# A two-layer diffusion trunk on one core: row sums of the modulations spread over the program, a wider apply of the norm, and caches loaded from another queue

## The chip, the cores and the metric

The kernel runs on one core of a Trainium2 chip, as one program and one launch. The metric is the device time of an execution in microseconds (us): here the median of three runs. The engines have short names below: PE is TensorE, DVE VectorE, ACT ScalarE, POOL GpSimd, SP SyncE. Each engine takes its instructions in the order in which the program issues them. A transfer is issued by the queue of an engine, and the issue stands in that engine's order like any other instruction.

## The reference

Two layers run over 128 context tokens and 128 latent tokens, with D = 1024 channels and D_FF = 2816. Each layer is two half feed-forward steps around a mixer:

```
x += 1/2 * gate1 * SwiGLU_1(mod1(RMSNorm(x)))
u  = mod2(RMSNorm(x)); z = u @ W_in
branches on z: differential attention, 2-D DFT, bidirectional chunkwise mLSTM
x += gate2 * (sum of gated branches @ W_out)
x += 1/2 * gate3 * SwiGLU_2(mod3(RMSNorm(x)))
modulation (shift, scale, gate) x 3 = SiLU(cond) @ W_ada + b_ada
```

`mod` is `x * (1 + scale) + shift`. The nine modulations of a layer are products of one vector for each token group with nine 1024 x 1024 blocks of `W_ada`. Latent tokens also read cached context keys and values (`cache_k`, `cache_v`) and seed the mLSTM from `state_C`. Everything is fp32, and the outputs are the two token groups, the new caches and the new states.

## The kernel before

All activations stay on chip, channels on the 128 partitions, both token groups side by side (256 columns). What moves is the weights, 1 MB chunks through six buffers called `raw`, each issued on SP's queue. A chunk is used as two or more **units** of 128x1024. Every unit is split into a high and a low part: ACT casts it (`whi`, L1473) and DVE subtracts the cast from the original (`wlo`, L1474). A product is then three matmuls, `hi*hi`, `lo*hi` and `hi*lo` (L167 to L169), so that PE, ACT and DVE all work on every unit. Splits are made up to six units ahead of use.

The program is a Python list, `steps`. A step has a function that issues its matmuls and follow-up work, and the units that it needs; the list's order is each engine's order. A layer has the parts ffn1 (22 blocks of the hidden width in 11 pairs, the "in" part, then four pairs of output channels, the "out" part), the mixer (queries first, then keys, values and the others, three branches, the output product), and ffn2.

Three places matter for the change.

**Modulations.** 16 of the 18 modulations are made while other parts run (the first two in `begin`). Seven are *row sums* on DVE: a chunk of the transposed weight is multiplied with the conditioning vector, broadcast over the partitions (`cb`), and summed over a row, in 16 instructions of 128x1024 per modulation (L339). Nine go through PE as *side steps*: 16 matmuls each, with the 32 columns of the conditioning vectors on the stationary side, two side steps a modulation (L164), and a `post` step of four transposes per part that has any. The table `ADA` (L42 to L47) gives for each part which modulations are row sums and which go through PE, and `spread_into` (L1288) spreads all of them evenly over the part's steps. Nearly all row sums stand in the "in" parts, since `spread_into` covers only these in an ffn.

**The norm.** `Norm` first makes `y = x * scale` block by block and splits it (`yh`, `yl`), so that the first four units of the next part can be multiplied by `y` before the norm's sum of squares is known. Then `stats`, `root` (a power on POOL), `diag` and `spread` make `bcs`, the reciprocal root for each token on all partitions, and `apply` (L478 to L491) makes `u = x * bcs * scale + shift` in eight blocks of 128x256, one multiplication on POOL (the first on DVE) and one half-block each on ACT and DVE, followed by a split into `uh` on ACT and `ul` on DVE. All units after the first four multiply by `u`.

**The start of a mixer.** After the queries' step, `loads2` (L676 to L682) issues three loads on POOL's queue: `cache_k` and `cache_v` into `ckv`, `state_C` into `C`. The attention's work runs as a lane, pieces of it issued between the matmuls of the following units: its first PE work is four transposes of `ckv` (L787), two and a half units after the first one that multiplies by `u`.

`begin` is ffn1 of the first layer: the first two modulations arrive in slabs (`ada(j)`, `channel(j)`) and the first three pairs are multiplied channel block by channel block.

Of the kernel before, what the change touches and what calls it, by code (L numbers as in the profile page):

```python
# [14 lines left out]
ALU = mybir.AluOpType  # L15
# [24 lines left out]
CT = 8  # L40
# [76 lines left out]
class Step:  # L117
    def __init__(self, fn, units=(), pump=True, lanes=False, ahead=()):
        self.fn, self.units, self.pump, self.lanes = fn, list(units), pump, lanes
        self.ahead = list(ahead)  # L120


@with_exitstack
def trunk_kernel(ctx: ExitStack, tc: tile.TileContext, a: dict):
# [89 lines left out]
    cb = const.tile([P, 2, D], F32, name="cb")  # L214
    maskb = const.tile([P, 2, P], BF16, name="maskb")
# [3 lines left out]
    run = {"lanes": False}  # L219
    late, held = [], []  # L220

    def add(fn, units=(), pump=True, ln=False, ahead=()):
        steps.append(Step(fn, units, pump, ln, ahead))

# [71 lines left out]

    def mod_steps(mods_):
# [4 lines left out]

        on_ve, mods_ = mods_
        st = {"left": 4 * len(mods_)}
        seq = []
# [12 lines left out]
        def finish(l, m, o, x):  # L318
            bT = parT[l][:, m * KD:(m + 1) * KD].unsqueeze(2).to_broadcast([P, KD, 2])
            ve.tensor_add(o, x, bT)  # L320
            if m % 3 == 1:
                k0 = 72 + m // 3 * KD
                gT = parT[l][:, k0:k0 + KD].unsqueeze(2).to_broadcast([P, KD, 2])
                ve.scalar_tensor_tensor(o, o, 1.0, gT, op0=ALU.add, op1=ALU.mult)
            elif m % 3 == 2 and m != 5:
                ve.tensor_scalar(o, o, 0.5, None, op0=ALU.mult)

        for i, (l, m) in enumerate(on_ve):
            o, junk = mods[l, m], []
            for j in range(KD // 2):  # L330
                ch = Chunk(a["w_adaT"][l, m, j], 2, D)
                for b in range(2):
                    for g in range(2):
                        u = Unit(ch, b, b + 1, 0, D, split=False)

                        def fn(u=u, k=2 * j + b, g=g, o=o, l=l, m=m, junk=junk):
                            if not junk:
                                junk.append(blk([P, D], "junkw"))
                            ve.tensor_tensor_reduce(junk[0], u.raw()[:, 0, :], cb[:, g, :], 1.0, 0.0,  # L339
                                                    op0=ALU.mult, op1=ALU.add, accum_out=o[:, k, g:g + 1])  # L340
                            if k == KD - 1 and g == 1:
                                finish(l, m, o, o)

                        seq.append(((i + (4 * j + 2 * b + g) / 16) / len(on_ve), fn, [u]))
        for i, (l, m) in enumerate(mods_):
            for j2 in range(2):
# [11 lines left out]
                seq.append(((2 * i + j2 + 0.4) / (2 * len(mods_)), fn, us))  # L358
        seq.sort(key=lambda x: x[0])
        out = [x[1:] for x in seq]  # L360
        if not mods_:
            return out

        def post():
# [12 lines left out]
            for i, (l, m) in enumerate(mods_):  # L377
                finish(l, m, mods[l, m], full[:, :, 2 * i:2 * i + 2])

# [4 lines left out]
    class Norm:  # L384
# [6 lines left out]
        def __init__(self, scale, shift):  # L391
            self.scale, self.shift = scale, shift
            self.y = self.sum = self.last = None
            self.ys = {}

        def begin(self):
            if self.scale is None:
                self.y = [blk([P, 4, 256], f"y{i}") for i in range(2)]
            else:
                self.y = ()  # L400
                self.yh = [blk([P, 4, 258], f"yh{i}", F32R) for i in range(2)]
                self.yl = [blk([P, 4, 258], f"yl{i}", F32R) for i in range(2)]
                self.shifts()
# [13 lines left out]
        def block(self, k):  # L417
# [6 lines left out]
            y = self.ys[k] = t2([P, 256], "y")  # L424
# [3 lines left out]
        def parts(self, k):  # L428
            if self.scale is not None:
                i, r = k // 4, k % 4  # L430
                hilo(self.ys.pop(k), self.yh[i][:, r, 0:256], self.yl[i][:, r, 0:256])
# [46 lines left out]
        def apply(self):  # L478
            U.h = [blk([P, 4, 256], f"uh{i}", F32R) for i in range(2)]
            U.l = [blk([P, 4, 256], f"ul{i}", F32R) for i in range(2)]  # L480
            vs = {}
            for k in range(KD + 1):
                if k < KD:
                    v = vs[k] = t2([P, 256], "v")
                    (po if k else ve).tensor_mul(v, xT[:, k, :], self.bc)
                    ac.activation(v[:, G[0]], v[:, G[0]], AF.Identity, scale=self.scale[:, k, 0:1],
                                  bias=self.shift[:, k, 0:1])
                    ve.tensor_scalar(v[:, G[1]], v[:, G[1]], self.scale[:, k, 1:2], self.shift[:, k, 1:2],  # L488
                                     op0=ALU.mult, op1=ALU.add)
                if k > 0:  # L490
                    hilo(vs.pop(k - 1), *uk(k - 1))  # L491
# [64 lines left out]
    def residual(k, ps, gate, norm):  # L556
# [26 lines left out]
    def add_ffn(l, which, norm, norm_next, mods_, begun=None):  # L583
        w_out = a[f"w_ffn{which}_out"][l]
        gate = mods[l, 2 if which == 1 else 8]
        hT = {}

        def h_tiles(j):
            i = j // 4
            if i not in hT:  # L590
                n = min(4, NF - 4 * i)
                hT[i] = (blk([P, n, 256], f"hh{i}", F32R), blk([P, n, 256], f"hl{i}", F32R))
# [24 lines left out]
        p0 = len(steps)  # L617
        for jj in range(n_pair):
            if jj == FIRST + 1 and l == 0 and which == 1:
                add(s_params2)  # L620
            if jj == 0:
# [923 lines left out]
```

## Time and profile before

| What | Value |
|---|---|
| time, median of 3 runs (lowest, highest) | 1352.44 us (1351.43, 1352.7) |
| the profiled execution's own time | 1352.04 us |
| its span, first to last instruction | 1350.3 us |
| PE busy | 1325.8 us, 98% of the span |
| DVE busy | 961.0 us, 71% |
| ACT busy | 683.5 us, 51% |
| POOL busy | 112.4 us, 8% |
| mean granted clock of TensorE | 0.996 |
| moved by DMA | 304.72 MB, 226 GB/s in the mean |

1.7 us of the profiled execution lie outside the span. The busy shares are means over parts that differ: in the "in" parts with row sums DVE is nearly full, in the "out" parts it is not. The matmuls are pipelined, so that their durations overlap; what one costs is read from the distance of two starts.

### The profile page before, as it was taken

The page shows a single profiled execution, that of the slowest core. Times are in us where ns is not written, and L with a number is a line of the kernel's source. Part 1 is how long each engine was busy: PE and PEld are TensorE (multiplying, and loading weights), DVE is VectorE, ACT ScalarE, POOL GpSimd, SP SyncE. Part 2 cuts the span into 40 slices and gives each one's busy share as a digit, 9 for nine tenths or more (in the row PEclk, how much of TensorE's full clock was granted, in tenths as well). Part 3 has the DMA queues.
Part 4 walks back from the last instruction along what each step waited for, and adds up shares of the span by engine and source line. Part 5 has one row for each costly group of instructions (what it writes and reads, how often), then busy time and mean ns, then how long its engine had stood idle before and what let it go on. Part 6 is the DMA issues. An engine that isn't in the chain of part 4 may idle for free.

```text
span 1350.3 us, 25902 instructions
## 1 busy us (share of the span) xinstructions
PE 1325.8 (98%) x10748; PEld 1257.2 (93%) x10748; DVE 961.0 (71%) x1535; ACT 683.5 (51%) x1097; POOL 112.4 (8%) x136
## 2 busy tenths in 40 slices
PE   8999999999999999999999999999999999999998
PEld 5899999788989998999999999998899899999998
DVE  4699866775557689977669976677565668886653
ACT  4564445665644465444455444456654445654441
POOL 2000003100000040000120000130000001200001
PEclk9999999999999999999999999999999999999999
DMA  9999864754588638987639886747446895477630
GB/s 366 339 342 320 289 191 148 219 183 129 172 287 304 221 126 282 312 303 234 197 125 304 305 297 201 200 146 218 132 152 226 294 303 163 153 259 236 216 100 32
DMA packets 220565, 304.72 MB, mean 226 GB/s; under 512 B 5584, under 2 KB 190176, under 8 KB 215712
## 3 DMA queue, kind: packets, MB, share of 16 engines
q1 hardware_dynamic: 216320, 295.93, 65.8%
q0 software_dynamic: 1680, 5.05, 1.1%
q10 hardware_dynamic: 2448, 2.10, 0.6%
q8 instruction: 84, 1.38, 0.4%
q14 instruction: 33, 0.27, 0.1%
HBM read 298.85 MB, written 3.15 MB: 224 GB/s over the span
## 4 chain that ended last, share of the span: by engine, by line
PE 83%; DVE 9%; ACT 3%; DMA 3%; issue 2%; ACTq 0%; POOL 0%; SPq 0%; DVEq 0%
PE pm L167 24%; PE pm L169 24%; PE pm L168 24%; PE pd L164 3%; DVE wlo L1474 3%; PE pb L164 2%; ACT whi L1473 2%; DVE v L488 2%; DMA raw<-w_ada 2%; DVE ul L179 1%; DVE junkw L339 1%; PE pa L164 1%; PE pm L736 1%; PE pm L738 1%; PE pm L737 1%
## 5 line engine op out<-in xcount | busy, mean ns | idle before, releaser
L1474 DVE TENSOR_TENSOR wlo<-raw,whi 128x1024 fp32r<-128x1024 f32 (+1 forms) x428 | 508.9, 1195 | 282.9 <-ACT whi L1473 275.2
L1473 ACT CAST whi<-raw 128x1024 fp32r<-128x1024 f32 (+1 forms) x428 | 434.9, 1025 | 336.3 <-PE pm L168 242.2
L167 PE MATMUL pm<-uh,whi 128*128 128x256 f32 x1904 | 545.2, 286 | 1.9 <-ACT uh L178 1.0
L169 PE MATMUL pm<-uh,wlo 128*128 128x256 f32 x1904 | 536.0, 282 | 4.9 <-DVE wlo L1474 4.9
L168 PE MATMUL pm<-ul,whi 128*128 128x256 f32 x1904 | 536.5, 282 | 1.8 <-DVE v L488 1.3
L167 PEld LDWEIGHTS pm<-uh,whi 128*128 128x128 f32 x1904 | 360.5, 189 | 20.9 <-issue 8.8
L169 PEld LDWEIGHTS pm<-uh,wlo 128*128 128x128 f32 x1904 | 358.8, 188 | 6.4 <-DVE wlo L1474 6.3
L168 PEld LDWEIGHTS pm<-ul,whi 128*128 128x128 f32 x1904 | 359.8, 189 | 4.3 <-DVE ul L179 1.9
L169 PE MATMUL pm<-hh,wlo 128*128 128x256 f32 x704 | 198.3, 282 | 0.0
L168 PE MATMUL pm<-hl,whi 128*128 128x256 f32 x704 | 197.8, 281 | 0.0
L167 PE MATMUL pm<-hh,whi 128*128 128x256 f32 x704 | 197.6, 281 | 0.0
L339 DVE CUSTOM_DVE_ANT_0 junkw<-raw,cb 128x1024 f32<-128x1024 f32 x112 | 136.5, 1219 | 0.1
L167 PEld LDWEIGHTS pm<-hh,whi 128*128 128x128 f32 x704 | 132.8, 189 | 0.0
L168 PEld LDWEIGHTS pm<-hl,whi 128*128 128x128 f32 x704 | 132.7, 188 | 0.0
L169 PEld LDWEIGHTS pm<-hh,wlo 128*128 128x128 f32 x704 | 132.5, 188 | 0.0
L413 POOL TENSOR_TENSOR nsum<-nsum,nsq 128x256 f32<-128x256 f32 x36 | 36.4, 1011 | 806.5 <-ACT nsq L411 806.5
L637 ACT ACTIVATE silu<-pm 128x512 f32<-128x512 f32 x38 | 22.7, 597 | 53.1 <-PE pm L169 53.1
L164 PE MATMUL pd<-raw,cT 128*32 128x512 f32 (+1 forms) x416 | 43.8, 533 | 4.9 <-DMA raw<-w_ada 4.9
L178 ACT CAST hh<-silu 128x512 fp32r<-128x512 f32 x41 | 25.3, 621 | 37.6 <-DVE silu L639 37.6
L558 DVE SCALAR_TENSOR_TENSOR xT<-pm,mod,xT 128x128 f32<-128x128 f32 x96 | 28.8, 342 | 17.9 <-PE pm L169 17.8
L1222 ACT ACTIVATE sig<-pm 128x512 f32<-128x512 f32 x24 | 14.4, 598 | 49.9 <-PE pm L169 49.8
L736 PE MATMUL pm<-whi,uh 128*128 128x512 f32 x96 | 39.3, 410 | 0.0
(337 smaller groups left out, 1755.5 us busy)
## 6 DMA issues: line engine op xcount, KB each, us to landing
raw<-w_ffn_in SPq DMA_DIRECT2D x82, 1024.0 KB, 7.1
raw<-w_ada SPq DMA_DIRECT2D x44, 1024.0 KB, 5.6
raw<-w_ffn_out SPq DMA_DIRECT2D x32, 1024.0 KB, 5.6
raw<-w_in SPq DMA_DIRECT2D x32, 1024.0 KB, 5.8
raw<-w_adaT SPq DMA_DIRECT2D x28, 1024.0 KB, 6.5
raw<-w_branch_gate SPq DMA_DIRECT2D x24, 1024.0 KB, 5.3
raw<-w_ffn_out SPq DMA_DIRECT2D x16, 768.0 KB, 4.6
raw<-w_out SPq DMA_DIRECT2D x8, 1024.0 KB, 6.3
```

Of the source, the lines that this page charges most:

```text
L164: pe.matmul(out, lhsT, rhs, start=start, stop=stop)
L167: pe.matmul(out, sh, mh, start=start, stop=False)
L168: pe.matmul(out, sh, ml, start=False, stop=False)
L169: pe.matmul(out, sl, mh, start=False, stop=stop)
L178: ac.copy(hi, src)
L339: ve.tensor_tensor_reduce(junk[0], u.raw()[:, 0, :], cb[:, g, :], 1.0, 0.0, op0=ALU.mult, op1=ALU.add, accum_out=o[:, k, g:g + 1])
L413: eng.tensor_add(self.sum, self.sum, sq)
L488: ve.tensor_scalar(v[:, G[1]], v[:, G[1]], self.scale[:, k, 1:2], self.shift[:, k, 1:2], op0=ALU.mult, op1=ALU.add)
L558: ve.scalar_tensor_tensor(xT[:, k, G[g]], ps[:, G[g]], gate[:, k, g:g + 1], xT[:, k, G[g]], op0=ALU.mult, op1=ALU.add)
L736: pe.matmul(ps[g], xh[:, G[g]], wh, start=(k == 0), stop=False)
L1473: ac.copy(u.hi, r)
L1474: ve.tensor_sub(u.lo, r, u.hi.bitcast(F32))
```

## The change

It has five parts.

1. Four modulations stay on PE, (0,2), (0,5), (0,8) and (1,5). Twelve are row sums (192 instead of 112 instructions). They are steps of their own now, placed by a rate per step that depends on the part (`RATE`): 0.93 and 0.85 in the "in" parts, 0.75 in the "out" parts, 0.3 to 0.5 in the mixer. The product that a row sum writes beside its sum goes to a fixed bf16 tile.
2. `y` is kept in fp32 in two tiles, and `apply` makes `u` from it in place: per half of the channels a multiplication by `bcs`, an addition of the shift, a cast on ACT and a subtraction, all 128x1024; POOL has no part in it.
3. In `begin`, `channel(k)` makes u in one fused pass, and the first one stands ahead of both splits of its step; the last slab's step splits one unit ahead of each hand-over.
4. `cache_k`, `cache_v` and `state_C` are loaded from ACT's queue.
5. The last tiles `hh` and `hl` of the hidden width share one tile; the columns that held padding for the side steps go (`CT`).

```diff
-ADA = {(0, "ffn1"): ([(0, 4), (0, 3)], [(0, 2)]),
-       (0, "mixer"): ([], [(0, 7), (0, 6), (0, 5)]),
-       (0, "ffn2"): ([(1, 1), (1, 0)], [(0, 8)]),
-       (1, "ffn1"): ([(1, 4), (1, 3)], [(1, 2)]),
-       (1, "mixer"): ([], [(1, 7), (1, 6), (1, 5)]),
-       (1, "ffn2"): ([(1, 8)], [])}
+CT = 0
+ADA = {(0, "ffn1"): [(0, 2)], (0, "mixer"): [(0, 5)], (0, "ffn2"): [(0, 8)], (1, "mixer"): [(1, 5)]}
+ROWS = [(0, 4), (0, 3), (0, 7), (0, 6), (1, 1), (1, 0), (1, 2), (1, 4), (1, 3), (1, 7), (1, 6), (1, 8)]
+RATE = {"in0": 0.93, "in": 0.85, "out": 0.75, "win": 0.3, "branch": 0.35, "last": 0.5, "merge": 0.0}
...
+    junkw = const.tile([P, D], BF16, name="junkw")
...
+                        def fn(u=u, k=2 * j + b, g=g, o=o, l=l, m=m):
+                            ve.tensor_tensor_reduce(junkw, u.raw()[:, 0, :], cb[:, g, :], 1.0, 0.0,
+                                                    op0=ALU.mult, op1=ALU.add, accum_out=o[:, k, g:g + 1])
...
         def apply(self):
             U.h = [blk([P, 4, 256], f"uh{i}", F32R) for i in range(2)]
             U.l = [blk([P, 4, 256], f"ul{i}", F32R) for i in range(2)]
-            vs = {}
-            for k in range(KD + 1):
-                if k < KD:
-                    v = vs[k] = t2([P, 256], "v")
-                    (po if k else ve).tensor_mul(v, xT[:, k, :], self.bc)
-                    ac.activation(v[:, G[0]], v[:, G[0]], AF.Identity, scale=self.scale[:, k, 0:1],
-                                  bias=self.shift[:, k, 0:1])
-                    ve.tensor_scalar(v[:, G[1]], v[:, G[1]], self.scale[:, k, 1:2], self.shift[:, k, 1:2],
-                                     op0=ALU.mult, op1=ALU.add)
-                if k > 0:
-                    hilo(vs.pop(k - 1), *uk(k - 1))
+            us = self.yf
+            bc = self.bc.unsqueeze(1).to_broadcast([P, 4, 256])
+            def times(i):
+                ve.tensor_mul(us[i], us[i], bc)
+            def plus(i):
+                v = us[i].rearrange("p k (g t) -> p k g t", g=2)
+                sh = self.shift[:, 4 * i:4 * i + 4, :].unsqueeze(3).to_broadcast([P, 4, 2, T])
+                ve.tensor_add(v, v, sh)
+                ac.copy(U.h[i], us[i])
+            def low_(i):
+                ve.tensor_sub(U.l[i], us[i], U.h[i].bitcast(F32))
+            times(0)
+            plus(0)
+            times(1)
+            low_(0)
+            plus(1)
+            low_(1)
...
-            po.dma_start(out=M["ck"][:, 0], in_=a["cache_k"][0, l].rearrange("h s d -> s h d"))
-            po.dma_start(out=M["ck"][:, 1], in_=a["cache_v"][0, l].rearrange("h s d -> s h d"))
+            nc.scalar.dma_start(out=M["ck"][:, 0], in_=a["cache_k"][0, l].rearrange("h s d -> s h d"))
+            nc.scalar.dma_start(out=M["ck"][:, 1], in_=a["cache_v"][0, l].rearrange("h s d -> s h d"))
             M["C0"] = blk([P, 2, H, P], "C0")
-            po.dma_start(out=M["C0"], in_=a["state_C"][0, l].rearrange("d h v k -> v d h k"))
+            nc.scalar.dma_start(out=M["C0"], in_=a["state_C"][0, l].rearrange("d h v k -> v d h k"))
...
-            ac.activation(x[:, G[0]], x[:, G[0]], AF.Identity, scale=sc[:, 0:1], bias=sh[:, 0:1])
-            ve.tensor_scalar(x[:, G[1]], x[:, G[1]], sc[:, 1:2], sh[:, 1:2], op0=ALU.mult, op1=ALU.add)
-            hilo(x, U.h[i][:, r, :], U.l[i][:, r, :])
+            x = t2([P, 256], "v0")
+            xh, xl = uk(k)
+            for g in range(2):
+                ve.scalar_tensor_tensor(x[:, G[g]], xT[:, k, G[g]], sc[:, g:g + 1], norm.bc[:, G[g]],
+                                        op0=ALU.mult, op1=ALU.mult)
...
             if j < KD:
-                split_one()
+                if j:
+                    split_one()
                 channel(j)
-                split_one()
+                while st["unit"] < 2 * j + 2:
+                    split_one()
             else:
+                pump_split(1)
                 done(0, ps[0])
...
+    todo, due = row_steps(), 0.0
+    for s in steps:
+        s.slot = []
+        due += s.rate
+        while due >= 1.0:
+            due -= 1.0
+            nxt = next(todo, None)
+            if nxt is not None:
+                s.slot.append(Step(*nxt))
+    steps[:] = [x for s in steps for x in (s, *s.slot)]
```

The change moves instructions at three places that the prediction speaks of. The first is ACT's order at the start of the first layer's mixer. `q` is the queries' last step, `whi` a weight split, `kl<-q` a later transfer of the attention. Before:

```order
L1473 CAST whi<-raw_2300 128x1024
L1473 CAST whi<-raw_2368 128x1024 x2
L696 ACTIVATE q<-ft,fc 128x128 x4
L1473 CAST whi<-raw_2426 128x1024 x2
L677 ACT_TABLE_LOAD
L1473 CAST whi<-raw_2484 128x1024
L716 COPY k<-pm 128x512
```

and now:

```order
L492 CAST uh_2815<-yf_2098 128x1024
L492 CAST uh_2816<-yf_2099 128x1024
L1523 CAST whi<-raw_2390 128x1024
L1523 CAST whi<-raw_2449 128x1024 x2
L720 ACTIVATE q<-ft,fc 128x128 x4
L1523 CAST whi<-raw_2508 128x1024 x2
L701 ACT_TABLE_LOAD
L703 DMA ckv<-cache_k 128x4x128
L704 DMA ckv<-cache_v 128x4x128
L706 DMA C_2882<-state_C 128x8x128
L1523 CAST whi<-raw_2518 128x1024
L740 COPY k<-pm 128x512
```

The three loads now stand in ACT's order behind three weight splits, the four queries, two more splits and a table load. The second place is POOL's order at the same point, before:

```order
L465 TENSOR_TENSOR rstd<-var,expo 128x2
L485 TENSOR_TENSOR v<-xT,bcs 128x256 x7
L679 DMA ckv<-cache_k 128x4x128
L680 DMA ckv<-cache_v 128x4x128
L682 DMA C_2898<-state_C 128x8x128
L684 MEMSET zgh 128x832
L685 MEMSET zgl 128x832
```

and now:

```order
L413 TENSOR_TENSOR nsum<-nsum,nsq 128x256
L465 TENSOR_TENSOR rstd<-var,expo 128x2
L708 MEMSET zgh 128x832
L709 MEMSET zgl 128x832
L1012 MEMSET gpk_3080 40x256
```

There the loads stood right behind the apply's seven multiplications, and POOL now has neither. The third place is DVE's order in the "out" part of the first layer's ffn1. `hl`, `yl` and `xT` are the hidden width, the next norm's y and the residual. Before:

```order
L558 SCALAR_TENSOR_TENSOR xT<-pm,mod_2_98,xT 128x128 x2
L1474 TENSOR_TENSOR wlo<-raw_1790,whi 128x768
L426 TENSOR_SCALAR y<-xT,mod_4_100 128x128
L179 TENSOR_TENSOR yl_2083<-y,yh_2081 128x256
L1474 TENSOR_TENSOR wlo<-raw_1855,whi 128x1024 x2
L1474 TENSOR_TENSOR wlo<-raw_1859,whi 128x1024 x2
L558 SCALAR_TENSOR_TENSOR xT<-pm,mod_2_98,xT 128x128 x2
```

and now (`ISA` with `junkw` is a row sum, the one without it reads the sum out):

```order
L319 ISA junkw,mod_7_103<-raw_2007,cb 128x1024
L319 ISA mod_7_103 128x1
L1524 TENSOR_TENSOR wlo<-raw_2131,whi 128x1024
L319 ISA junkw,mod_7_103<-raw_2007,cb 128x1024
L319 ISA mod_7_103 128x1
L1524 TENSOR_TENSOR wlo<-raw_2131,whi 128x1024
L319 ISA junkw,mod_7_103<-raw_2199,cb 128x1024
L319 ISA mod_7_103 128x1
L1524 TENSOR_TENSOR wlo<-raw_2202,whi 128x1024 x2
```

Row sums now stand between the weight splits of this part. From the one order to the other the row sums of the parts go, in the order of the program, from 28 to 25 (ffn1 in), 4 to 19 (out), 0 to 21 (mixer), 29 to 29 and 3 to 18 (ffn2), and in the second layer from 29 to 29, 3 to 19, 0 to 21, 14 to 11 and 2 to 0.

## Rows read from the trace of the kernel before

**Rows 1.** Page, busy time of each engine and the chain that ended last.
```profile
PE 1325.8 (98%) x10748; PEld 1257.2 (93%) x10748; DVE 961.0 (71%) x1535; ACT 683.5 (51%) x1097; POOL 112.4 (8%) x136
PE 83%; DVE 9%; ACT 3%; DMA 3%; issue 2%; ACTq 0%; POOL 0%; SPq 0%; DVEq 0%
```

**Rows 2.** Timeline of PE at one side step: start, us, engine, line, operation, tiles.
```profile
583.67 0.28 PE L169 MATMUL pm<-uh,wlo 128*128 128x256 f32 x1
583.88 1.92 PE L164 MATMUL pd<-raw,cT 128*32 128x512 f32 x16
585.73 0.39 PE L167 MATMUL pm<-uh,whi 128*128 128x256 f32 x1
```

**Rows 3.** Timeline of PE, the side step that waits for its chunk, and what follows.
```profile
723.17 1.07 PE L164 MATMUL pd<-raw,cT 128*32 128x512 f32 x8
725.65 1.07 PE L164 MATMUL pd<-raw,cT 128*32 128x512 f32 x8 [1.41 <-DMA raw<-w_ada]
726.64 0.38 PE L167 MATMUL pm<-uh,whi 128*128 128x256 f32 x1
```

**Rows 4.** Stretches: window, length, busy us (instructions) PE, PEld, DVE, ACT, POOL, PEclk, DMA, GB/s.
```profile
63.00:147.00 84.00, 82.74 (x692) 79.10 (x693) 79.91 (x113) 46.36 (x53) 0.00 (x0) 1.00 0.96 334
...
609.70:674.00 64.30, 64.30 (x546) 64.30 (x545) 42.57 (x69) 30.71 (x44) 4.86 (x5) 1.00 0.65 209
```

**Rows 5.** Timeline of DVE, a row sum and the split behind it.
```profile
73.20 1.22 DVE L339 CUSTOM_DVE_ANT_0 junkw<-raw,cb 128x1024 f32<-128x1024 f32 x1
74.34 1.22 DVE L1474 TENSOR_TENSOR wlo<-raw,whi 128x1024 fp32r<-128x1024 f32 x1
```

**Rows 6.** Timeline of PE in `begin` and at its hand-over to the fourth pair.
```profile
14.30 1.07 PE L164 MATMUL pd<-raw,cT 128*32 128x256 f32 x16 [1.16 <-DMA raw<-w_ada]
16.41 0.38 PE L167 MATMUL pm<-uh,whi 128*128 128x256 f32 x1 [1.04 <-ACT uh L178]
63.01 0.38 PE L167 MATMUL pm<-uh,whi 128*128 128x256 f32 x1 [0.91 <-ACT whi L1473]
64.27 0.39 PE L169 MATMUL pm<-uh,wlo 128*128 128x256 f32 x1 [0.76 <-DVE wlo L1474]
```

**Rows 7.** Timeline of PE at the start of the first ffn2.
```profile
507.18 0.39 PE L169 MATMUL pm<-uh,wlo 128*128 128x256 f32 x1 [0.76 <-DVE wlo L1474]
```

**Rows 8.** Timeline of the first mixer's start on PE: first unit with u, transposes of ckv.
```profile
236.00 0.29 PE L167 MATMUL pm<-uh,whi 128*128 128x256 f32 x1
246.90 0.60 PE L172 MATMUL pa<-cst,ckv 128*128 128x128 f32 x4
```

**Rows 9.** The same on DVE: first and last instruction of apply, and one in between.
```profile
229.79 0.95 DVE L485 TENSOR_TENSOR v<-xT,bcs 128x256 f32<-128x256 f32 x1
236.14 2.14 DVE L488 TENSOR_SCALAR v<-v,mod,mod 128x128 f32<-128x128 f32 x1
240.41 0.43 DVE L179 TENSOR_TENSOR ul<-v,uh 128x256 fp32r<-128x256 f32 x1 [0.49 <-ACT uh L178]
```

**Rows 10.** The same on POOL and ACT: the load's issue and the table load.
```profile
235.74 0.83 POOL L679 DMA_DIRECT2D ckv<-cache_k  x1
249.77 1.28 ACT L677 ACT_TABLE_LOAD   x1
```

**Rows 11.** Tile ckv, from issue to landing, us.
```profile
DMA to landing us min/median/max: 3.4/3.7/3.8
```

**Rows 12.** Page, issues: tiles, queue, count, KB each, median us to landing.
```profile
kl<-q ACTq DMA_DIRECT2D x8, 64.0 KB, 5.7
```

**Rows 13.** Timeline of PE in the second mixer: first unit with u, a pause, transposes of ckv.
```profile
895.52 0.28 PE L167 MATMUL pm<-uh,whi 128*128 128x256 f32 x1
...
902.14 0.39 PE L169 MATMUL pm<-uh,wlo 128*128 128x256 f32 x1 [0.76 <-DVE wlo L1474]
...
907.79 0.60 PE L172 MATMUL pa<-cst,ckv 128*128 128x128 f32 x4
```

**Rows 14.** The stretch ahead of these transposes (columns as in rows 4).
```profile
902.00:906.00 4.00, 3.86 (x20) 3.86 (x21) 3.93 (x11) 1.52 (x3) 0.00 (x0) 0.58 0.65 156
```

More of the change, by code (lines that the diff above doesn't have):

```diff
@@ L223, in add @@
         steps.append(Step(fn, units, pump, ln, ahead))
+        steps[-1].rate = run["rate"]
     def pump_lanes(which=(0, 1, 2)):
@@ L294, in x_in, with finish, row_steps @@
                 (ac.copy if g and not k4 else ve.tensor_copy)(xT[:, 4 * k4:4 * k4 + 4, G[g]], t)
+    def finish(l, m, o, x):
+        bT = parT[l][:, m * KD:(m + 1) * KD].unsqueeze(2).to_broadcast([P, KD, 2])
+        ve.tensor_add(o, x, bT)
+        if m % 3 == 1:
+            k0 = 72 + m // 3 * KD
+            gT = parT[l][:, k0:k0 + KD].unsqueeze(2).to_broadcast([P, KD, 2])
+            ve.scalar_tensor_tensor(o, o, 1.0, gT, op0=ALU.add, op1=ALU.mult)
+        elif m % 3 == 2 and m != 5:
+            ve.tensor_scalar(o, o, 0.5, None, op0=ALU.mult)
+    def row_steps():
+        for l, m in ROWS:
+            o = mods[l, m]
+            for j in range(KD // 2):
+                ch = Chunk(a["w_adaT"][l, m, j], 2, D)
+                for b in range(2):
+                    for g in range(2):
+                        u = Unit(ch, b, b + 1, 0, D, split=False)
+                        def fn(u=u, k=2 * j + b, g=g, o=o, l=l, m=m):
+                            ve.tensor_tensor_reduce(junkw, u.raw()[:, 0, :], cb[:, g, :], 1.0, 0.0,
+                                                    op0=ALU.mult, op1=ALU.add, accum_out=o[:, k, g:g + 1])
+                            if k == KD - 1 and g == 1:
+                                finish(l, m, o, o)
+                                known.add((l, m))
+                        yield fn, [u]
+    known = set()
     def mod_steps(mods_):
-        on_ve, mods_ = mods_
         st = {"left": 4 * len(mods_)}
-        seq = []
+        out = []
         def side(tiles, f0, f1):
@@ L316, in side @@
                 ac.copy(st["ev"], st["ps"])
[L318 to L344, printed above, removed]
         for i, (l, m) in enumerate(mods_):
@@ L356, in fn @@
                               for e in range(2) for c in range(2)], 0, 512)
[L358 to L362, printed above, removed]
+                out.append((fn, us))
         def post():
@@ L402, in begin @@
                 self.yl = [blk([P, 4, 258], f"yl{i}", F32R) for i in range(2)]
+                self.yf = [blk([P, 4, 256], f"yf{i}") for i in range(2)]
                 self.shifts()
@@ L554, in prod8, with residual @@
                 mid()
-    def residual(k, ps, gate, norm):
+    def residual(k, ps, gate, norm, of):
+        assert of <= known, (of, known)
         for g in range(2):
@@ L585, in add_ffn @@
         gate = mods[l, 2 if which == 1 else 8]
+        of = {(l, 2), (l, 3), (l, 4)} if which == 1 else {(l, 8), (l + 1, 0), (l + 1, 1)}
+        of = {x for x in of if x[0] < DEPTH}
         hT = {}
@@ L590, in h_tiles @@
             if i not in hT:
[L591 to L592 removed]
+                if NF - 4 * i <= 2:
+                    t = blk([P, 4, 256], f"hhl{i}", F32R)
+                    hT[i] = (t[:, 0:2, :], t[:, 2:4, :])
+                else:
+                    hT[i] = (blk([P, 4, 256], f"hh{i}", F32R), blk([P, 4, 256], f"hl{i}", F32R))
             return hT[i]
@@ L643, in add_ffn @@
         p1 = len(steps)
+        run["rate"] = RATE["out"]
         ks = [(0, 8), (8, 16), (16, 22)]
@@ L647, in add_ffn @@
             ps = [None, None]
+            if mp == 3:
+                run["rate"] = 0.0
             for k0, k1 in ks:
@@ L1228, in drain @@
                             pass
+                    if bi == 2:
+                        run["rate"] = RATE["last"]
                     add(drain)
+                if bi == 2 and mq == 1:
+                    run["rate"] = 0.0
                 for p in range(2):
@@ L1282, in fn @@
                     prod8(p_, u, mk_)
-                    residual(m, p_, gate, norm_next)
+                    residual(m, p_, gate, norm_next, of)
                 add(fn, [us_[i]], pump=mp < 3)
-        spread_into(p0, len(steps) - 8, mods_)
+        if mods_:
+            spread_into(p0, len(steps) - 8, mods_)
         return loads
@@ L1369, in slice_ @@
                 norm.spread()
-                for i in range(2):
-                    v.append(blk([P, 4, 256], f"v{i}"))
-                    for r in range(4):
-                        (po if i or r else ve).tensor_mul(v[i][:, r, :], xT[:, 4 * i + r, :], norm.bc)
             else:
@@ L1405, in trunk_kernel @@
     for l in range(DEPTH):
-        add_ffn(l, 1, norms[l, 0], norms[l, 1], ADA[l, "ffn1"], begin if l == 0 else None)
+        add_ffn(l, 1, norms[l, 0], norms[l, 1], ADA.get((l, "ffn1")), begin if l == 0 else None)
         pos = len(steps)
-        steps.insert(pos - 6, Step(add_mixer(l, norms[l, 1], norms[l, 2], ADA[l, "mixer"]), pump=False))
-        add_ffn(l, 2, norms[l, 2], norms[l + 1, 0], ADA[l, "ffn2"])
+        steps.insert(pos - 6, Step(add_mixer(l, norms[l, 1], norms[l, 2], ADA.get((l, "mixer"))), pump=False))
+        add_ffn(l, 2, norms[l, 2], norms[l + 1, 0], ADA.get((l, "ffn2")))
     def fin():
@@ L1429, in trunk_kernel @@
     add(fin)
+    todo, due = row_steps(), 0.0
[8 more added lines that the diff above has]
+    steps[:] = [x for s in steps for x in (s, *s.slot)]
+    assert next(todo, None) is None
     units, need, floor = [], {}, 0
```

37 lines of the change are left out of this document (25 added, 12 removed).

## The prediction, made blind

> **What bounds the kernel now.** The page comes first: PE is busy 98% of the span, and most of the chain that ended last is PE's matmuls [rows 1]. So a change gains where it takes work from PE or ends a pause of PE, and it costs where it makes one. DVE is second, but its 71% is a mean, and for this change the stretches tell more: between 63 and 147 us, an "in" part with row sums, DVE is busy 79.91 of 84.00 us (95%) and PE still 82.74; in an "out" part (609.7 to 674) DVE is busy 42.57 of 64.30 us, and PE all of it [rows 4]. Then the timelines of PE at the places that the change touches: a side step, the start, and the starts of the parts. A price is read there as the distance of two starts: 546 matmuls in 64.30 us [rows 4] are one every 0.118 us.
>
> **Side work that leaves PE.** PE had nine modulations and keeps four, so five go, two side steps each: ten. Around one, the last product starts at 583.67 and the next at 585.73 [rows 2]: 2.06 us, less the 0.118 that lies between two products anyway, is 1.94, and ten are 19.4 us. All of it was on the path, since PE had no pause in that stretch. One of the ten also waits for its chunk: from 723.17 to 726.64 are 3.47 us [rows 3], where the undisturbed step takes 1.85 from its own start [rows 2]; 1.6 more goes. The one post step that goes too is left out of the sum, as a fraction of one side step. Together **-21.0 us**.
>
> **Row sums that DVE gets.** 80 more, each 1.14 us from its start to the next one's [rows 5], 91 us of DVE. They cost only where DVE is not done in time. The "in" parts hardly change (28 to 25, 29 to 29). Three "out" parts get about 15 more: 42.57 + 15 x 1.14 = 59.7 us of 64.3 or 93%, the share at which DVE stood between 63 and 147 us. PE lost 1.26 us there in 84 [rows 4], and 0.76 of that is the pause at 64.27 [rows 6], so that the full DVE itself showed little loss. For three parts of 64 us the bounds are nothing and 3 x 64 / 84 x 1.26 = 2.9; the sixteen to twenty rows more in each mixer, where the trace has no stretch like it, go with them. I take the upper part, since a row sum that waits for its chunk also holds the splits behind it: **+2.0 us**. Their chunks: four more of 1 MB in 64 us are 65 GB/s on top of 209, and 334 were moved without harm [rows 4]. The bf16 junk tile I cost at nothing.
>
> **The start.** In `begin` the first product stands 1.04 us behind the cast of u [rows 6]; with channel 0 ahead of the two splits this pause goes, if the chunk that ended PE's wait at 14.30 comes no later. At the hand-over PE waits 0.91 for a cast and 0.76 for a low part [rows 6], and a split made one unit earlier takes both away. Sum 2.7; bounds nothing (what follows is late by as much) and 5 (a steadier start also saves the slow matmuls after the pauses, as many again). **-2.7 us.**
>
> **The norm's apply at the ffn parts.** Three ffn parts start with a pause like that at 507.18, where PE waits 0.76 us for a low part that DVE makes after apply [rows 7]. Six wide instructions instead of its many small ones end earlier, but u's second half is ready only at their end. Half of each pause, **-1.2 us**; bounds 0 and 3 x 0.76 = 2.3.
>
> **The mixers' starts.** This term decides the sum. Before, the loads of the caches were issued on POOL at 235.74 [rows 10] and landed 3.4 to 3.8 us later [rows 11], at about 239.3. The transposes that read them started at 246.90 [rows 8], so nobody waited for them. PE was there so late because it met DVE's pauses: from 236.00, the 60 matmuls of two and a half units at 0.118 need 7.1 us, and 10.9 passed [rows 8]. Now the three issues stand on ACT's queue behind the queries, two more splits and the table load. The table load started at 249.77 [rows 10], long after the transposes' old start. What pulls it forward is the faster apply. DVE's first instruction of it stays where bcs allows, at 229.79 [rows 9]; six of 128x1024 at 1.14 us, the split's and row sum's pace [rows 5], take 6.8, and about 1.2 goes in waits for the two casts on ACT: 237.9, against 240.84 for the end of the last one before [rows 9]. 2.9 us earlier then come the splits, the queries and the table load: it starts near 246.9, ends 1.28 us later at 248.15, and the cache's issue stands there. Its landing on ACT's queue is not in the trace for this size: 3.7 us were needed from POOL's queue [rows 11], 5.7 for a small transfer from ACT's own queue [rows 12]. Between them I take 4.7: **252.85**, 6.0 us later than before. PE, in order, has only units behind these transposes, and with its faster apply gets there at about 243.7; it stands for 9 us.
> In the second mixer the same way takes 252.85 - 236.00 = 16.85 us from the first unit with u, where 12.27 were needed before [rows 13]: +4.6. Ahead of those transposes lies a stretch with PE at a granted clock of 0.58 of full, in which 20 matmuls took 4.0 us [rows 14] instead of 20 x 0.118 = 2.4; PE had paused for DVE at 902.14, 0.76 us [rows 13]. A pause of 9 us should bring PE to its lower level (1.2 of 2.4 GHz) in the same way, 1.6 us in each mixer, 3.3 together. The sum of the mixers is 6.0 + 4.6 + 3.3 = **+13.9 us**. The bounds: landing 3.7 or 5.7 (1 us either way in each), no slow clock (3.3 less), DVE another microsecond later (2 more).
> A page of the Trainium skill sees the move the other way: SBUF — State Buffer, section SBUF: two separate sides, says that transfers issued from POOL starve of descriptors while DVE holds a shared port, and that one should issue from ACT or SP instead. The trace bears out that something is held: DVE's instruction of 128x128 at 236.14 took 2.14 us while POOL issued, one of twice the size at 229.79 took 0.95 [rows 9]; yet the transfer had landed 7 us before its use. By that rule alone the loads would come sooner and the term would be nothing or a gain. Against it stands DMA: Bandwidth & Descriptors, section Rules for kernel authors: issue a transfer early and wait for it late. Here the issue moves about 12 us later, and the trace speaks for this rule.
>
> **Sum.** -21.0 + 2.0 - 2.7 - 1.2 + 13.9 = -9.0. The profiled execution took 1352.04, 0.4 under the median: 1343.0, or 1343.4 at the median's level. I forecast **1343**. With every bound on the good side (begin -5, ffn -2.3, DVE 0, mixers 13.9 - 5.3 = 8.6) it is -19.7, 1332; with every one on the bad side (0, 0, +2.9, 13.9 + 4) it is -0.2, 1352.
>
> **Rivals.**
> *The caches come in time.* If the issue can pass on ACT's queue ahead of the splits, or the transposes come later than I count, the wait is gone. PE would reach the transposes at 243.7 instead of 246.90, 3.2 sooner, and in the second mixer 4.6 sooner: -21.0 + 2.0 - 2.7 - 1.2 - 7.8 = -30.7, **1321**. For it speaks that apply and POOL no longer hold each other; against it the order on ACT's queue, where a load that must land by 243.7 must be issued by 240. Chance 0.10.
> *VectorE becomes the bound in the "out" parts (slower).* There 64.3 - 42.57 = 21.7 us are free, so that 15 more rows may cost 1.45 us each; above that PE waits for the low parts, and from 9.0 / 45 = 0.2 more, 1.65 us each, the gain of all the rest is eaten up. What could lengthen them is a chunk that is late and holds DVE, as the side step's was by 1.4 us [rows 3]. At twice 1.14, 45 x 0.83 = 37 us are lost: **1380**. Against it: 95% of DVE cost PE nothing for 84 us. Chance 0.05.
> *The sum of the small terms fails.* The start and the ffn parts bring nothing and the caches land late: the bad end above, **1351**. Chance 0.08.
> The forecast itself has 0.77. Inside it the lower clock after the wait may be absent: 1340.
>
> **Range and chances.** 1328 to 1351 us. The likeliest case's own range is 1332 to 1350; below it lies some of the case where the caches come in part in time. What a measurement of this kernel can tell from no change is 0.2%, 1349.7 to 1355.1. Faster: 0.77 less a little of its upper edge, and 0.10: 0.85. Same: 0.09, mostly the third rival. Slower: 0.06.
>
> **What would show it.** Side steps: 8 groups of 16 matmuls with 32 columns instead of 18. Row sums: 192, mean still near 1.2 us, "out" parts with DVE above 90% and PE without pauses for low parts. Start: the first product near 15.4 us. Mixers: a pause of PE of 8 to 10 us ahead of the transposes of ckv, ended by a transfer of ACT's queue, and a granted clock under 0.7 behind it, in both layers. The forecast is wrong if that pause is missing or under 4 us (then the time is near 1325), or if PE waits for low parts in the "out" parts.

## The result, and the profile after

The changed kernel takes **1339.91 us** (median of 4 runs, 1339.12 to 1340.87), beside 1352.57 for the kernel before on the same chip: a ratio of 0.9906, 95% interval 0.9889 to 0.9923. The forecast was 1343, with a range of 1328 to 1351. Its span is 1338.4 us, 11.9 less.

First the page: busy time of each engine, row sums, and splits [rows 1].

```profile
PE 1306.4 (98%) x10584; PEld 1256.4 (94%) x10584; DVE 1038.2 (78%) x1652; ACT 659.8 (49%) x1026; POOL 68.0 (5%) x88
...
L319 DVE CUSTOM_DVE_ANT_0 junkw<-raw,cb 128x1024 bf16<-128x1024 f32 x192 | 233.7, 1217 | 0.0
```

PE has 164 instructions fewer and DVE is busy 77 us more. A row sum still takes 1.22 us, with its bf16 output too. In an "out" part, which answers to [rows 4], and behind the transposes of ckv (columns as there):

```profile
126.00:190.00 64.00, 64.00 (x544) 64.00 (x543) 57.03 (x93) 30.44 (x41) 2.67 (x3) 1.00 0.76 254
243.60:248.00 4.40, 4.35 (x21) 4.38 (x22) 2.73 (x5) 2.15 (x3) 0.00 (x0) 0.50 1.13 327
899.60:904.00 4.40, 4.40 (x23) 4.40 (x22) 2.81 (x4) 2.00 (x3) 0.00 (x0) 0.50 1.11 320
```

DVE fills the "out" part to 89%, and PE has no pause there. In both mixers PE runs at a granted clock of 0.50 behind the wait for ckv, its lower level, called the half clock below. The mixers' starts, which answer to [rows 8, 10, 13], on PE, on ACT's queue and on ACT:

```profile
231.14 0.28 PE L166 MATMUL pm<-uh,whi 128*128 128x256 f32 x1
...
243.65 1.09 PE L171 MATMUL pa<-cst,ckv 128*128 128x128 f32 x4 [4.93 <-DMA ckv<-cache_k]
...
899.01 1.09 PE L171 MATMUL pa<-cst,ckv 128*128 128x128 f32 x4 [4.67 <-DMA ckv<-cache_k]
```

```profile
238.84 0.40 ACT L720 ACTIVATE q<-ft,fc 128x128 f32<-128x128 f32 x1 [0.32 <-DVE ft L552]
238.97 0.39 ACTq L703 DMA_DIRECT2D ckv<-cache_k  x1
239.15 1.03 ACT L1523 CAST whi<-raw 128x1024 fp32r<-128x1024 f32 x1
239.38 0.53 ACTq L704 DMA_DIRECT2D ckv<-cache_v  x1
239.95 0.52 ACTq L706 DMA_DIRECT2D C<-state_C  x1
240.09 1.04 ACT L1523 CAST whi<-raw 128x1024 fp32r<-128x1024 f32 x1
241.14 1.28 ACT L701 ACT_TABLE_LOAD   x1
```

The load is issued at 238.97, while the last query has just begun on ACT; the two splits and the table load, which stand ahead of it in the program, run after it. The last query had waited for DVE until 238.82, and the issue follows within 0.15 us: so ACT's queue seems to wait for what the instructions ahead of it wait for; for their work it did not wait. The order of the program, in which the issue stands behind them, is not the order in time. The transposes start 4.7 us after the issue (4.4 in the second mixer, where the issue is at 894.62).

Two pauses of PE were not in the forecast. The first stands ahead of the matmul that spreads the norm's root, in both mixers: PE, DVE and POOL there.

```profile
222.00 0.67 PE L163 MATMUL pb<-dg,ones 128*128 128x256 f32 x2 [1.16 <-DVE yf L426]
```

```profile
220.33 1.52 DVE L469 TENSOR_SCALAR dg<-cst,rstd 128x128 f32<-128x128 f32 x1 [0.28 <-POOL rstd L465]
220.53 1.39 DVE L426 TENSOR_SCALAR yf<-xT,mod 128x128 f32<-128x128 f32 x1
...
220.25 0.78 POOL L708 MEMSET zgh<- 128x832 f32 x1
220.99 0.78 POOL L709 MEMSET zgl<- 128x832 f32 x1
```

`dg` takes 0.28 us elsewhere; here it ends when POOL's second memset does (221.85 and 221.77). The second pause is the remaining side step in the first ffn2:

```profile
524.87 1.07 PE L163 MATMUL pd<-raw,cT 128*32 128x512 f32 x8 [1.58 <-DMA raw<-w_ada]
528.74 1.94 PE L163 MATMUL pd<-raw,cT 128*32 128x512 f32 x8 [2.81 <-DMA raw<-w_ada]
530.60 0.58 PE L166 MATMUL pm<-uh,whi 128*128 128x256 f32 x1
```

Both kernels issue the same 9744 weight products in the same order, so the lead of the changed one can be read product by product. Starts of the same product:

| Product | Place | before | after | lead |
|---|---|---|---|---|
| 0 | first product | 16.41 | 15.15 | 1.3 |
| 240 | in `begin` | 56.14 | 53.07 | 3.1 |
| 320 | behind the hand-over | 67.91 | 62.93 | 5.0 |
| 1600 | start of the first mixer | 225.76 | 219.72 | 6.0 |
| 1760 | behind the wait for ckv | 249.68 | 248.80 | 0.9 |
| 3280 | end of the first mixer | 488.40 | 481.99 | 6.4 |
| 4800 | end of the first ffn2 | 677.11 | 675.76 | 1.3 |
| 6460 | start of the second mixer | 882.89 | 873.02 | 9.9 |
| 6660 | behind the wait for ckv | 915.30 | 908.85 | 6.5 |
| 8160 | end of the second mixer | 1150.19 | 1138.70 | 11.5 |
| 9600 | last "out" part | 1323.57 | 1311.62 | 12.0 |

### The profile page after: what moved, and what is told of

Same layout as the page of the kernel before. It is cut to its first block, busy times and chain, and to the rows that moved or that the text cites. A ratio compares the mean times of both kernels' runs of the same rounds, so it can differ in the third digit from the quotient of the medians.

```text
span 1338.4 us, 25512 instructions
## 1 busy us (share of the span) xinstructions
PE 1306.4 (98%) x10584; PEld 1256.4 (94%) x10584; DVE 1038.2 (78%) x1652; ACT 659.8 (49%) x1026; POOL 68.0 (5%) x88
## 5 line engine op out<-in xcount | busy, mean ns | idle before, releaser
L319 DVE CUSTOM_DVE_ANT_0 junkw<-raw,cb 128x1024 bf16<-128x1024 f32 x192 | 233.7, 1217 | 0.0
L168 PE MATMUL pm<-hh,wlo 128*128 128x256 f32 x640 | 179.6, 281 | 0.0
L166 PE MATMUL pm<-hh,whi 128*128 128x256 f32 x640 | 179.5, 280 | 0.0
L167 PE MATMUL pm<-hl,whi 128*128 128x256 f32 x640 | 179.5, 280 | 0.0
L168 PEld LDWEIGHTS pm<-hh,wlo 128*128 128x128 f32 x640 | 120.7, 189 | 0.0
L166 PEld LDWEIGHTS pm<-hh,whi 128*128 128x128 f32 x640 | 120.6, 188 | 0.0
L167 PEld LDWEIGHTS pm<-hl,whi 128*128 128x128 f32 x640 | 120.5, 188 | 0.0
L411 ACT ACTIVATE nsq<-xT 128x256 f32<-128x256 f32 x42 | 17.5, 417 | 53.2 <-DVE xT L570 53.1
L761 PE MATMUL pm<-wlo,uh 128*128 128x512 f32 x96 | 37.9, 395 | 0.0
```

Of the source, the lines that this page charges most:

```text
L166: pe.matmul(out, sh, mh, start=start, stop=False)
L167: pe.matmul(out, sh, ml, start=False, stop=False)
L168: pe.matmul(out, sl, mh, start=False, stop=stop)
L319: ve.tensor_tensor_reduce(junkw, u.raw()[:, 0, :], cb[:, g, :], 1.0, 0.0, op0=ALU.mult, op1=ALU.add, accum_out=o[:, k, g:g + 1])
L761: pe.matmul(ps[g], xh[:, G[g]], wl, start=False, stop=False)
```

## The experiments

Ratios are to the kernel before on the same chip. Theory A puts the wait for ckv on the place of the issue, B and C on the queues themselves.

**The loads back on POOL's queue** (all else as changed):

```diff
-            nc.scalar.dma_start(out=M["ck"][:, 0], ...)
+            po.dma_start(out=M["ck"][:, 0], ...)
```

> The changed kernel with the three cache loads of each mixer back on POOL's queue, all else as changed. Theory A (the wait for ckv, 5.1 and 4.8 us in the two mixers, comes from the place of the issue on ACT, behind the queries): POOL now issues right behind the norm's root, some 15 us ahead of use, both waits vanish and with them the half clock behind them, about 2 us each: 13 to 14 us less than the changed kernel's 1339.9, so near 1326. POOL's issues (0.8 us each, 2.4 us) fall where DVE makes dg, so that PE's pause there may grow from 1.2 to 2.5 us in each mixer: then 1328 to 1329. Rival B (POOL's transfers are starved while DVE works, so that ACT's queue is the better one): ckv lands late from POOL too, or DVE's apply is held as in the kernel before, and the time is 1337 or more.

Measured 1328.57 us (0.9805, 0.9782 to 0.9828). Both waits and the half clock behind them are gone, as A has it. What POOL does to DVE showed too, in another instruction than named; PE, DVE and POOL of this run:

```profile
240.76 0.60 PE L171 MATMUL pa<-cst,ckv 128*128 128x128 f32 x4
...
220.16 0.28 DVE L469 TENSOR_SCALAR dg<-cst,rstd 128x128 f32<-128x128 f32 x1 [0.28 <-POOL rstd L465]
220.36 2.22 DVE L426 TENSOR_SCALAR yf<-xT,mod 128x128 f32<-128x128 f32 x1
...
220.09 0.81 POOL L703 DMA_DIRECT2D ckv<-cache_k  x1
220.89 0.75 POOL L704 DMA_DIRECT2D ckv<-cache_v  x1
221.63 0.90 POOL L706 DMA_DIRECT2D C<-state_C  x1
```

`dg` is short, but the next of its kind is held until POOL's third issue ends, and PE pays 1.7 us for it later in the first mixer (two pauses, at the first unit with u). Behind these two pauses, of 0.64 and 0.88 us, it ran at a granted clock of 0.58 from 234 to 238 us, which cost 1.5 us more.

**The loads on ACT's queue, ahead of the mixer's first step:**

```diff
-        add(lambda: first(norm, us, q_done), us, pump=2)
+        add(lambda: (caches(), first(norm, us, q_done)), us, pump=2)
```

> The changed kernel with the same three loads on ACT's queue, but issued ahead of the mixer's first step instead of behind the queries. Theory A (the place of the issue): no wait for ckv, no half clock behind it, 13 to 14 us less than the changed kernel, near 1326; three issues of 0.4 to 0.5 us in front of y's last blocks on ACT cost 0 to 1.4 us of PE in each mixer. Rival C (ACT's queue itself lands late, 4.7 us or more, or the transfers compete with the weights): a wait of several us for ckv is left, and the time stays above 1335.

Measured 1328.31 us (0.9812, 0.9796 to 0.9829). ACT's queue issues at 217.64, and PE passes the transposes without a pause:

```profile
217.64 0.39 ACTq L702 DMA_DIRECT2D ckv<-cache_k  x1
...
238.37 0.60 PE L171 MATMUL pa<-cst,ckv 128*128 128x128 f32 x4
```

Either queue will do if the issue is early: A holds, B and C fall. The gain is 11.6 us where A had 13 to 14. Product by product, 5.5 and 5.2 us come back at the transposes, but 1.2 and 2.9 are paid at the next wait of the same lane, for the context keys from ACT (`kctx`). That the two runs agree to 0.3 us is partly chance: each median is of four executions that differ by 4 to 7 us, and their small losses lie at different places.

**The kernel before with only its loads on ACT's queue** (`po` to `nc.scalar` in the three lines):

> The kernel before with only its three cache loads moved to ACT's queue. Theory A: ACT issues them right behind the last query, whose instruction on ACT starts at 247.46 in the kernel before; landing 4.7 us later at about 252.3, where the transposes started at 246.90: 5.4 us in the first mixer, 4 in the second, and about 2 us of half clock behind each wait, less up to 1.5 us each that DVE gains where POOL's issues held it: +10 to +13 us, 1363 to 1365. Theory of the prediction as written (issue behind the table load that started at 249.77): landing at 255.7, +18 to +20 us, 1371 or more. Rival C (the queue makes no difference by itself): 1352.

Measured 1363.09 us (1.0067, 1.0052 to 1.0082): 10 us slower by this edit alone, within A's numbers. The version of the prediction, with an issue behind the table load, is excluded: the issue came at 247.68, the table load at 249.85. Not all is as A has it: behind the pause of 3.19 us in the first mixer the granted clock stayed at 1.00, and only behind the one of 5.60 in the second it fell.

```profile
247.55 0.40 ACT L696 ACTIVATE q<-ft,fc 128x128 f32<-128x128 f32 x1 [0.31 <-DVE ft L541]
247.68 0.39 ACTq L679 DMA_DIRECT2D ckv<-cache_k  x1
...
249.85 1.28 ACT L677 ACT_TABLE_LOAD   x1
...
252.39 0.63 PE L172 MATMUL pa<-cst,ckv 128*128 128x128 f32 x4 [3.19 <-DMA ckv<-cache_k]
```

**POOL's memsets later in the program** (a step `gate_weights` behind the keys holds the two memsets and the casts):

> The changed kernel with POOL's two memsets (zgh, zgl) and the casts behind them moved from the step behind the queries to the step behind the keys. Theory D (PE's pause of 1.3 us before the matmul that spreads the norm's root, new in both mixers, comes from DVE's dg being held for 1.5 us by these memsets, which POOL now reaches right behind the root): dg takes 0.28 us as elsewhere, the pause goes, and all behind it is 1.2 us earlier in each mixer: 2 to 2.5 us less than the changed kernel, 1337.5. Rival E (dg is late for another reason, such as the wider y tiles): pause and time as in the changed kernel, 1339.9.

Measured 1341.12 us (0.9899, 0.9872 to 0.9926). It told nothing about D: POOL had nothing to do in between, so its memsets ran as early as before, `dg` still took up to 1.53 us, and the casts in their new place cost PE 1.6 us in each mixer. A step's place orders an engine's work; it doesn't delay it.

**The memsets on DVE instead** (early loads as above; `po.memset` to `ve.memset`):

> The run with the early loads on ACT's queue (1328.3 us), and in addition the two memsets of zgh and zgl on DVE, behind the norm's apply, instead of on POOL. Theory D (PE's new pause of about 1.2 us before the matmul that spreads the norm's root comes from POOL's memsets holding DVE's dg): dg takes 0.28 us in both mixers, the pause goes, 2 us less in all: 1326. DVE pays 0.5 to 0.9 us per mixer for the memsets behind the queries, which PE sees only if a low part is late there. Rival E (dg is late for another reason): dg above 1 us and 1328 again.

Measured 1333.49 us (0.9849, 0.9831 to 0.9867). `dg` takes at most 0.29 us and PE's pause ahead of the spread shrinks by 1.11 us in both mixers, as D says. The time still rose by 5 us. Product by product, 1.2 and 0.5 us are paid back in the two mixers behind the memsets, 0.3 each at the first unit with u, and at the side step of the first ffn2 PE waited 2.7 us longer for its chunk, with more of the slow clock behind it.

**The modulation (0,8) in the first mixer's side steps:**

```diff
-ADA = {..., (0, "mixer"): [(0, 5)], (0, "ffn2"): [(0, 8)], ...}
+ADA = {..., (0, "mixer"): [(0, 5), (0, 8)], ...}
```

> The former run's kernel, with the modulation (0,8), the gate of the first ffn2, made by two side steps in the first mixer instead of in that ffn2's in part. Theory F (in the changed kernel PE waits there near 523 us for the side step's second chunk, because DVE, busy all the time with splits and row sums, frees the buffers late and SP issues the chunk late; 7.5 us for a step of 1.9, and 0.8 of half clock behind it): the wait goes, and the steps cost 1.95 each where they come to stand: 5 us less than the former run, 1321. Rival G (the wait is handed on to another chunk): less than 2 us.

Measured 1324.37 us (0.9791, 0.9777 to 0.9806), 9.1 less than the former run (1333.49). The step near 523 us loses 8.7 us of PE time, the other one 1.9, and the two cost 1.94 and 1.95 in the mixer. The wait belongs to that place; G falls. That the buffers were freed late is the likely reason, but only the place was varied.

**Other places for the row sums** (rates `out` 0.85, `win` 0.2):

> The former run's kernel with other rates for the row sums: out 0.85 instead of 0.75, win 0.2 instead of 0.3; by that no row sum stands within three instructions ahead of the softmax's reciprocal or the scaling of ha on DVE in either mixer. Theory H (PE's longer waits in the mixers, 1.8 for pc and 0.8 to 1.1 for ha against 0.7 and nothing before, are one row sum of 1.14 us each that stands right ahead of the lane's work on DVE): about 4 us less than the former run, 1317. Rival I (the lanes are late since DVE is full, wherever the rows stand, or the out parts at 95% now make PE wait): no less, or more.

Measured 1322.42 us (0.9775, 0.9759 to 0.9790), 2 us less than the former run (1324.37), which is about the spread of these runs. Like `pc`, `ha` is a tile of a lane that DVE makes and PE transposes. At ha, PE's pauses went where a row sum went; its transposes in the former run and in this one:

```profile
1068.64 0.66 PE L171 MATMUL pb<-cst,ha 128*128 128x128 f32 x4 [0.89 <-DVE ha L1194]
```

```profile
1062.55 0.60 PE L171 MATMUL pb<-cst,ha 128*128 128x128 f32 x4
```

Product by product, 0.35, 0.3 and 1.1 us went at ha. Ahead of pc the pause shrank by 0.8 us in the first mixer and grew by 0.25 in the second. In all that is about half of what was expected, and the last run below shows that the 0.8 was not the row sum's place. The "out" part at 58.18 of 64 us of DVE still shows no pause of PE.

**The first part of the change undone** (112 row sums, ten side steps more; also two buffers instead of four for one small tile of the attention, to make room):

> The changed kernel with the first part undone: seven modulations as row sums (112 instructions, nearly all in the in parts, 0.4 per step in the out parts until they run out, none in the mixers), nine through PE, that is ten side steps more; everything else as changed, the caches' loads too. By the sum: ten times 1.94 us and a post step back, 20 us, less the waits behind row sums in the mixers (4.6 us of pauses, 1 to 3 of half clock): 1352 to 1356. If row sums cost PE also in the ffn parts, then less than 1350; if they cost nothing in the mixers, 1360.

Measured 1357.1 us (1.0032, 1.0017 to 1.0047), 17 us above the changed kernel and slower than the kernel before. In the mixers the sum holds to a tenth: side steps of 1.94 to 2.03 come back, and five pauses of 1.16, 0.88, 1.14, 0.31 and 1.11 us behind row sums go, 4.6 in all. With the two pauses ahead of pc the lower clock behind them goes too (granted clock 0.64 and 0.66 in the changed kernel, 1.00 here), 1.5 us each. Above the range it is by one more side step's chunk that came late (5.7 us for a step of 1.9, near 727), and 1.1 us at a granted clock of 0.70 behind it. So the change without its first part would have been a loss.

**The third part alone, on the kernel before:**

> The kernel before with the third part alone: begin as in the changed kernel (one fused pass per channel, the first one ahead of both splits, a split ahead of each hand-over). The prediction had -2.7 us for it. Compared product by product, the changed kernel is 3.1 us ahead behind the start and 5.0 behind the hand-over; the 1.9 us above the prediction would be the half clock between 18 and 22 us, which it does not show. By that: -5 us, 1348. If the other parts had a share in it (no multiplications on POOL, other row sums): -2.7 us or less, 1350 or more.

Measured 1349.68 us (0.9971, 0.9960 to 0.9982). Its lead is 3.4 us at product 240 and 5.3 behind the hand-over, as in the changed kernel; 4.1 of it are left at the end of the profiled run and 3.6 in the median. The time alone does not decide, since its interval reaches from 2.4 to 5.4 us of gain; the lead behind the hand-over does. The half clock, before and in this run (columns as in [rows 4]):

```profile
18.00:20.00 2.00, 1.72 (x9) 1.72 (x10) 1.87 (x4) 0.09 (x1) 0.83 (x1) 0.65 1.06 423
20.00:22.00 2.00, 2.00 (x11) 2.00 (x11) 1.07 (x4) 1.57 (x3) 0.00 (x0) 0.50 1.02 413
```

```profile
18.00:20.00 2.00, 2.00 (x20) 2.00 (x18) 1.42 (x6) 1.42 (x3) 0.00 (x0) 1.00 1.09 435
20.00:22.00 2.00, 2.00 (x26) 1.28 (x25) 0.73 (x1) 0.64 (x2) 0.00 (x0) 1.00 0.95 380
```

PE's pauses of 1.16 and 1.04 us ahead of this stretch [rows 6] were followed by the lower level before. In this run PE is busy 1.91 of the 2 us from 14 to 16, before it was 1.07, and the clock stayed up.

**Other places, and the memsets on POOL again:**

> The run with the row sums' other places (1322.4), but with the two memsets on POOL again, as in the changed kernel. By theory D the pause of 1.1 us behind dg comes back in both mixers: 1324 to 1325. If what DVE pays for the memsets (a later split behind the queries) costs PE as much, the time is the same, 1322; the run with the memsets on DVE, which got slower by 5 us for other reasons, did not tell.

Measured **1320.92 us** (0.9766, 0.9753 to 0.9779). The pause behind dg is back, 1.1 us in each mixer, and about as much is saved behind the queries: a tie. DVE's order ahead of pc is that of the run before, but PE's pauses there are as long as in the changed kernel; the run before, and this one:

```profile
277.43 1.12 PE L171 MATMUL pa<-cst,pc 128*128 128x128 f32 x4 [0.82 <-DVE pc L875]
```

```profile
275.77 1.26 PE L171 MATMUL pa<-cst,pc 128*128 128x128 f32 x4 [2.02 <-DVE pc L875]
...
918.85 1.12 PE L171 MATMUL pa<-cst,pc 128*128 128x128 f32 x4 [1.63 <-DVE pc L875]
```

In the run before PE itself came later in the first mixer, by a pause of 2.00 us and a granted clock of 0.62 between 255 and 264 us. In both runs DVE is busy about 11.4 of the last 11.9 us ahead of these transposes, with one row sum in them. So at pc the full stretch of DVE counts and not the row sum's place in it, as rival I has it; only at ha did the place matter. Of all versions run this is the fastest: the change with early loads on ACT's queue, (0,8) in the mixer, and the other rates.

## Why the prediction was right, and by how much its terms were off

- **Side steps, -21.0, and row sums, +2.0.** Undoing the part cost 17.2 us, where these terms give 19.0, but that they agree is partly luck. Each side step was worth 1.94 to 2.03, as forecast. The row sums cost PE nothing in the "out" parts, as taken from [rows 4]; they cost in the mixers, where the trace had no stretch like it: each is 1.14 us long, and PE waits up to that long where one stands right ahead of a lane's instruction on DVE (ha) or in a full stretch of DVE ahead of one (pc). Five such pauses make 4.6 us and the lower clock behind two of them 2.9, 7.5 in all, and only 2.0 were in the sum. In the undone version a side step's chunk came later than in the kernel before (5.7 us and 1.1 of lower clock, against 3.5 us), which hides much of the difference.
- **The start, -2.7.** Mis-sized: 5.0. The pauses were right, and the half clock behind them came on top; the bound of 5 had been given for it.
- **The ffn parts' starts, -1.2.** Mis-sized: about 3.0, beyond the bound of 2.3. At each of the three starts the pause for the low part went and a shorter one for u's second half came, and the lead grew by about 1.0 us (5.8 to 6.8, 1.5 to 2.4, 11.5 to 12.5).
- **The mixers' starts, +13.9.** The mechanism was right: a pause ahead of ckv's transposes, ended by a transfer of ACT's queue, and the lower clock behind it, in both layers. Its size was 5.1 and 3.4 us in the two (leads of 6.0 and 0.9, 9.9 and 6.5), 8.5 in all, with the pause behind dg in it. The step that failed is "it starts near 246.9, ends 1.28 us later at 248.15, and the cache's issue stands there": ACT's queue did not wait for the table load. From the first unit with u the issue came after 7.8 us, not 12.2. The work ahead of it was forecast well: the table load ended 11.3 us after that unit. Of the 4.3 us between, 3.4 are thus the wait for that work, which did not exist. The landing of 4.7 us and PE's arrival (7.4 us after that unit, 7.7 forecast) were right, so that PE waited 4.9 instead of 9. The lower clock behind the two waits cost 2.0 and 1.9 us, a little more than the 3.3 in the sum.
- **Not in the sum.** The pause behind dg, 1.2 and 1.15 us. The side step in the first ffn2: it takes 7.5 us more than the products there took before, and the other step of that pair lies elsewhere than before; the lead falls by 5.1 us over this ffn2. The forecast named late chunks as a hazard for row sums on DVE; it was PE that waited, for the chunk of a side step that stayed.
- **The rivals.** The caches in time: 1321 was the price named for it, and with early loads the kernel takes 1328.3; the rest is what the sum did not hold, and 1320.9 is reached without the late chunk and with the other places. VectorE as the bound of the "out" parts did not occur. The net error of 3 us is small by luck. It hides 5.4 us in the mixers' starts, 2.3 in the start and 1.8 in the ffn parts' starts on the good side, against 5.5 for the row sums and about 5.5 for the late chunk. The rest, some 4 us on the good side in smaller places, was not taken apart.
- **The two rules.** The Trainium skill's DMA: Bandwidth & Descriptors, section Rules for kernel authors (issue early, wait late), agrees with this case: the move of the issue, not of the queue, cost the time (1363.09 against 1353.36, and 1339.91 against 1328.31). The Trainium skill's SBUF — State Buffer, section SBUF: two separate sides, has it that DVE instructions of certain kinds (in a two-port mode, or with two inputs in SBUF against a GpSimd instruction that reads it) and GpSimd instructions lock each other out of a shared pair of ports for a whole instruction. DVE's 0.28 us that became 1.52 beside memsets and 2.22 beside three issues agree with a block of that sort, though no run shows the kind of DVE's instruction, and it lasted through two memsets and three issues in a row. The advice of the same section to change the queue gave nothing by itself (1328.57 and 1328.31 from either queue).

## What to carry to other kernels

Moving a load to another engine's queue moves its issue to that engine's place in the program: look first at what that queue waits for ahead of it, and place the load early; here two runs with early issue from different queues came within 0.3 us of each other, and late issue cost 10 to 12. Work that is spread over an engine with room to spare is free only where that engine has time left before the next instruction on which the bound engine waits. Look at the stretch ahead of each such instruction: where it is full, as ahead of pc, moving the work by a place gains nothing. Aligning two traces product by product turns a net gain of 12 us into its parts, of which three were losses.

## What the runs showed of the hardware

- ACT's queue issued a transfer 2.2 us before a table load began that stands ahead of it in the program (238.97 against 241.14).
- The same load took 0.39 us of ACT's queue to issue where POOL took 0.83 [rows 10]. The transfers into ckv landed 4.7 to 5.0 us after a late issue on ACT's queue (changed kernel), 3.7 to 3.9 after an early one on the same queue, and 3.4 to 3.6 from POOL's queue (the changed kernel with its loads back there).
- A DVE instruction of 128x128 that takes 0.28 us took 1.52 beside POOL's memsets and 2.22 beside its DMA issues.
- After pauses of 4.93 and 4.67 us TensorE ran at a granted clock of 0.50 for the following 4.4 us; where the pauses went, so did that. One long pause is no sure sign: behind one of 3.19 us the clock stayed at 1.00, and behind two of 0.64 and 0.88 us within 2 us it fell to 0.58.
